# Layer A's turned probabilities: sixteen transfers inside the on-chip memory per half, and the products with v ahead of the next queries

## The chip, the cores and the metric

The kernel runs on one core of one Trainium2 chip. The metric is the device time of one execution in microseconds (us). The core has five engines that run their own instruction streams: TensorE (PE, matrix products), VectorE (DVE), ScalarE (ACT), GpSimd (POOL) and SyncE (SP, which here only issues transfers). Sixteen DMA engines move the data. Each engine takes its instructions in order, so an instruction that waits holds up all that stand behind it on the same engine.

## The reference

One layer A (dilated window attention, three groups) and one layer B (neighbourhood attention) on 512 rows of width 1024. The part that matters here is layer A's attention of each head:

```
logits = einsum('brhqd,brhkd->brhqk', qb, kb) * scale + bias
logits = where(valid, logits, NEG_INF)
mx = max(logits, axis=-1);  p = exp(logits - mx)
denom = sum(p, axis=-1)
out = einsum('brhqk,brhkd->brhqd', p, vb) / denom
...
y = sum(alpha * out over the three groups) * silu(gate);  x = x + y @ w_out
```

The probabilities p come out with the queries on the partitions. For the product with v the keys have to be on the partitions, so p is turned.

## The kernel before

Layer A works on eight pairs of heads (hc = 0 to 7, `NHC`). Two Python generators are woven into one program. `main` holds the projections: for each hc a fixed list of weight blocks, each 128 x 1024 float32 (512 KB), is loaded into one of nine buffers `wraw` (L256, on SP's queue), split into a rounded part `wh` (ACT, L133) and the rest `wl` (DVE or POOL in turns, L137), and multiplied in three products per block (PE, L286, `acc`). A block's half of 512 columns is a "job" here: 6 products for a mixed block, 12 for the blocks of the gate and of v. The projections of q and k are mixed from four blocks b11, b21, b12, b22 in a scheme with sums; some sums of weights are made by transfers that add to a buffer, issued from POOL (L184), and by POOL itself (L177). Each hc has 32 jobs: 0 to 3 b11, 4 and 5 gate, 6 to 9 b21, 10 to 13 b11 with b12 added to it, 14 to 17 a sum t2, 18 to 21 b22, 22 to 25 b12 with b22 added to it, 26 and 27 v, 28 to 31 t2 with b21 added to it. For the next hc they go on at 0.

`side` holds the attention: `q_a` (four groups of transposes of `rawq`, the projected queries and keys), `k_a` (`rawk`), `attn_a` (scores `log`, softmax `p`, turning, products with v `o`). PE's order is fixed where the generators weave: a clock that counts PE's work (`clock`) decides when `side` takes its next step, and `later_on` puts a job (a transfer) at a distance on that clock. The order on the other engines is made by a scheduler's own estimate of times; `keep_in_program_order` pins an instruction against others of its engine.

A pair of heads is done in two halves u = 0, 1 of 256 queries. For each half, DVE turns blocks of 32 x 32 within their 32 partitions (`turner.put`, L850, into the tile `tr`, of which there is one buffer). The blocks must then change partitions: block row a of 32 partitions, part b of the columns, goes to partitions 32b to 32b + 31. `turner.send` does it through DRAM: four writes `td<-tr` of 256 KB (L859), and 8500 units of the clock later four reads `pt<-td` of 256 KB (L863), 1300 units apart, all on SP's queue. Layer B uses the same class with 224 KB, for all but its last two pairs. When all reads of u = 1 are issued, `stamp` holds ("pt", hc, 1); 6000 units later `weigh` makes the products with v (`o<-pt`: 48 products), and `put_y` multiplies by the gate and stores y (`y_d<-gt`, L779).

For hc up to 6 the steps after the scores are: load the next biases (`bias_a`, L813 and L818), `v_a` (transposes of `vt`), `q_a(hc + 1)`, wait for ("pt", hc, 1), `weigh`. Before `main` allocates the next `rawq` it asks for `q_a` to have been done (`yield "q", hc - 1`). At hc = 6, y of the first pairs is read back (`yr<-y_d`, L798) into the buffer `tr`, and ACT rounds it (L804). hc = 7 turns its probabilities on PE and has no such transfers.

The lines that the scheduler and `order` name: a transfer on SP's queue waits for its buffers and also for the transfer eight places earlier on that queue.

Of the kernel before, what the change touches and what calls it, by code (L numbers as in the profile page):

```python
# [46 lines left out]
def tile_hybrid_encoder(  # L47
# [13 lines left out]
    nc = tc.nc  # L61
# [216 lines left out]
    clock = [0.0]  # L278
# [27 lines left out]
    def later_on(delay, job):  # L306

        timers.append((clock[0] + delay, job))
        timers.sort(key=lambda t: t[0])
# [529 lines left out]
    class turner:  # L839
# [12 lines left out]
        def send(self, dst, wait, pace, key=None):  # L852
# [15 lines left out]
            for b in range(4):  # L868
                later_on(pace * b, partial(write, b))
                later_on(wait + pace * b, partial(read, b))  # L870

    def attn_a(hc):
        e0, e12 = st.pop(("e", hc))
        q0h, q0l, q12, k0h, k0l = st.pop(("q", hc))
# [101 lines left out]
        if hc < NHC - 1:  # L976
            for u in range(2):
                turned = turner(512)
                turners.append(turned)
                for hd, t, pr in scores(u):  # L980
                    turned.put(pr, 512, 256 * hd + 128 * (t % 2))
                key = ("pt", hc, u)
                later_on(10000, partial(turned.send, pq[:, 2048 * u : 2048 * u + 2048], 8500, 1300, key))
                yield 9500
            if hc + 1 < NHC:
                st["e", hc + 1] = bias_a(hc + 1)
            yield from v_a(hc)
            yield from q_a(hc + 1)
            yield "wait", ("pt", hc, 1), 6000
            if hc < NHC - 2:  # L990
                put_y(hc, weigh(), True, False)
                yield
                return
            back = y_back(range(4), "tr")
            yield "wait", ("rawk", hc + 1), 0
            put_y(hc, weigh(), True, False)
            for n in range(4):
                y_split(back, n, n)
            yield "wait", ("q", hc + 1), 0
            back = y_back(range(4, NHC - 2), "rawq")  # L1000
            yield 4000
            for n in range(4, NHC - 2):
                y_split(back, n - 4, n)
        else:
            for u in range(2):
                held = scores(u)
                yield 4000
                for args in held:
                    turn_p(*args)
                    yield  # L1010
            yield from v_a(hc)
            yield "wait", ("gate", hc), 500
            stamp["ya", "turned"] = 0
            put_y(hc, weigh(), True, True)
            yield
# [386 lines left out]
```

## Time and profile before

| | |
|---|---|
| time, median of 3 runs | 948.82 us (945.91 to 950.09) |
| the profiled execution: its time | 949.64 us |
| its span, first to last instruction | 947.8 us |
| mean granted clock of TensorE | 0.951 |
| PE busy | 851.6 us, 90% |
| DVE, ACT, POOL busy | 613.8, 506.4, 354.3 us |
| moved by all transfers | 153.84 MB |
| HBM read, written | 126.41 MB, 26.40 MB |

Layer A's projections and attention take the span up to about 600 us, its output projection follows, and layer B runs from about 700 us. In a view of windows the row of a stretch gives its length, then for PE, PEld, DVE, ACT and POOL the busy time with the number of instructions, then the granted clock of TensorE, the share of DMA engine time, and GB/s. In a timeline a row is start, duration, engine, line, operation, output and inputs, and in brackets the idle time before it with what ended it. SPq is SP's queue: the time there is that of issuing.

### The profile page before, as it was taken

The numbers are of one execution on the slowest core, as the hardware profiler recorded it, in microseconds if no ns is written. First come the engines' busy times: TensorE is split into PE (matmuls) and PEld (weight loads), VectorE is DVE, ScalarE is ACT, GpSimd is POOL, SyncE is SP. The second block draws the span as 40 slices with busy tenths as digits, with TensorE's granted clock in tenths as the row PEclk, the third lists the DMA queues.
The fourth block names the chain that finished last, engine by engine and source line by source line (L and its number), as shares of the span: only waits on it lengthen the run. The fifth ranks groups of instructions, "written<-read, shape, count | busy, mean of one in ns | idle before, by whom it ended". The sixth has DMA issues, their size and how long they took to land.

```text
span 947.8 us, 15692 instructions
## 1 busy us (share of the span) xinstructions
PE 851.6 (90%) x5475; PEld 693.5 (73%) x5475; DVE 613.8 (65%) x1563; ACT 506.4 (53%) x1058; POOL 354.3 (37%) x328
## 2 busy tenths in 40 slices
PE   7957989996996996996996995999999999999998
PEld 5746767784774774775774774788999888888876
DVE  7776766872783684684585584753856776666743
ACT  6535654852752763663663663553546666544641
POOL 6346335534454443444453452411122223213411
PEclk9879999997997998997998998899999999999999
DMA  9252389698598488498498498126526554455212
GB/s 346 86 123 45 115 240 201 175 246 174 141 249 179 136 249 177 126 246 189 115 236 200 105 236 232 50 75 216 184 78 184 151 162 136 133 182 153 87 45 90
DMA packets 66911, 153.84 MB, mean 162 GB/s; under 512 B 7184, under 2 KB 24528, under 8 KB 66704
## 3 DMA queue, kind: packets, MB, share of 16 engines
q1 hardware_dynamic: 60496, 130.80, 46.8%
q0 software_dynamic: 6048, 22.02, 12.6%
q8 instruction: 43, 0.70, 0.3%
q14 instruction: 36, 0.29, 0.1%
q10 hardware_dynamic: 288, 0.01, 0.0%
HBM read 126.41 MB, written 26.40 MB: 161 GB/s over the span
## 4 chain that ended last, share of the span: by engine, by line
PE 49%; DMA 16%; ACT 12%; DVE 12%; issue 6%; POOL 3%; SPq 2%; DVEq 0%; ACTq 0%; POOLq 0%
PE acc L286 39%; DMA wraw<-in_w 10%; ACT wh L133 4%; PE o L286 4%; PE tp L290 3%; DMA td<-tr 3%; PE log L286 2%; ACT p L941 2%; ACT p L760 2%; DVE wl L137 2%; POOL wl L137 2%; ACT p L1198 1%; SPq L818 1%; DMA pt<-td 1%; DVE tr L850 1%
## 5 line engine op out<-in xcount | busy, mean ns | idle before, releaser
L137 POOL TENSOR_TENSOR wl<-wraw,wh 128x512 fp32r<-128x512 f32 (+1 forms) x167 | 221.3, 1334 | 391.1 <-ACT wh L133 370.5
L133 ACT CAST wh<-wraw 128x512 fp32r<-128x512 f32 (+1 forms) x360 | 211.8, 593 | 251.1 <-PE acc L286 243.1
L137 DVE TENSOR_TENSOR wl<-wraw,wh 128x512 fp32r<-128x512 f32 (+1 forms) x193 | 155.3, 808 | 159.0 <-ACT wh L133 155.9
L286 PE MATMUL acc<-wl,hn_h 128*128 128x384 f32 (+1 forms) x488 | 183.9, 377 | 45.4 <-POOL wl L137 44.7
L286 PE MATMUL acc<-wh,hn_h 128*128 128x384 f32 (+1 forms) x488 | 190.2, 390 | 3.0 <-DVE gt L1121 2.6
L286 PE MATMUL acc<-wh,hn_l 128*128 128x384 f32 (+1 forms) x488 | 182.1, 373 | 0.0
L286 PEld LDWEIGHTS acc<-wl,hn_h 128*128 128x128 f32 x488 | 95.3, 195 | 58.6 <-POOL wl L137 49.5
L286 PEld LDWEIGHTS acc<-wh,hn_h 128*128 128x128 f32 x488 | 95.3, 195 | 19.4 <-DVE gt L1121 4.2
L286 PEld LDWEIGHTS acc<-wh,hn_l 128*128 128x128 f32 x488 | 95.2, 195 | 10.2
L286 PE MATMUL acc<-wl,mix_h 128*128 128x512 f32 x224 | 90.5, 404 | 8.0 <-DVE wl L137 4.2
L286 PE MATMUL acc<-hn_h,wh 128*128 128x512 f32 x192 | 80.0, 417 | 11.7 <-ACT wh L133 11.4
L286 PE MATMUL acc<-wh,mix_h 128*128 128x512 f32 x224 | 88.8, 396 | 0.4 <-ACT wh L133 0.4
L286 PE MATMUL acc<-wh,mix_l 128*128 128x512 f32 x224 | 88.0, 393 | 0.0
L286 PE MATMUL acc<-hn_h,wl 128*128 128x512 f32 x192 | 76.1, 396 | 1.6 <-DVE wl L137 1.6
L286 PE MATMUL acc<-hn_l,wh 128*128 128x512 f32 x192 | 75.9, 395 | 0.0
L760 ACT ACTIVATE p<-p,mn 128x512 f32<-128x512 f32 (+3 forms) x128 | 70.9, 588 | 2.1 <-DVE mn L759 2.1
L184 POOL DMA_DIRECT2D wraw<-in_w x42 | 38.7, 996 | 82.4 <-DMA wraw<-in_w 77.2
L850 DVE STREAM_TRANSPOSE tr<-p 128x512 f32<-128x512 f32 (+1 forms) x80 | 54.9, 686 | 19.4 <-ACT p L760 14.3
L941 ACT ACTIVATE p<-p,mn 128x512 f32<-128x512 f32 (+1 forms) x64 | 44.9, 702 | 41.2 <-DVE mn L930 41.0
L286 PEld LDWEIGHTS acc<-wl,mix_h 128*128 128x128 f32 x224 | 42.4, 189 | 24.3 <-DVE wl L137 8.2
L286 PEld LDWEIGHTS acc<-hn_h,wh 128*128 128x128 f32 x192 | 36.6, 191 | 22.5 <-ACT wh L133 11.7
L372 DVE TENSOR_REDUCE ss<-sq 128x4 f32<-128x256 f32 (+1 forms) x96 | 47.3, 501 | 7.5 <-POOL sq L371 3.9
(158 smaller groups left out, 1470.7 us busy)
## 6 DMA issues: line engine op xcount, KB each, us to landing
wraw<-in_w SPq DMA_DIRECT2D x95, 512.0 KB
wraw<-in_w POOLq DMA_DIRECT2D x42, 512.0 KB, 7.9
wraw<-in_w SPq DMA_DIRECT2D x38, 384.0 KB
td<-tr SPq DMA_DIRECT2D x56, 256.0 KB
pt<-td SPq DMA_DIRECT2D x56, 256.0 KB
td<-tr SPq DMA_DIRECT2D x24, 224.0 KB
pt<-td SPq DMA_DIRECT2D x24, 224.0 KB
e<-l_d SPq DMA_DIRECT2D x32, 112.0 KB
```

Of the source, the lines that this page charges most:

```text
L133: nc.scalar.copy(h, raw)
L137: eng.tensor_sub(l, raw, h.bitcast(F32))
L184: lambda: nc.gpsimd.dma_start(dst.tile, src(), accum_op=ALU.add)
L286: nc.tensor.matmul(o, l, r, **kw)
L290: nc.tensor.transpose(o, i, ident)
L372: nc.vector.tensor_reduce(ss[:, i * ns : (i + 1) * ns], sq.rearrange("p (a b) -> p a b", b=64), axis=AX.X, op=ALU.add)
L760: nc.scalar.activation(pr, pr, AF.Copy, scale=mn[:, 3:4])
L818: nc.sync.dma_start(e12[:, 2 * hd + g, :], bass.AP(l12_d.tensor, l12_d.offset + h * 512 + 256 * g + 31, [[0, 4], [-1, 32], [1, 224]]),)
L850: nc.vector.transpose(dst, src[:, :n].rearrange("p (i b k) -> p i b k", b=4, k=32))
L941: nc.scalar.activation(row, row, AF.Exp, bias=mn[:, 1:2], scale=-1.0, accum_out=mn[:, 2:3])
L1198: nc.scalar.activation(pr[:, o : o + n], pr[:, o : o + n], AF.Exp, bias=mn[:, 0:1], scale=-1.0, accum_out=mn[:, 2:3])
```

## The change

Layer A no longer calls `turner.send`. A new method `move` moves each 32-partition block of `tr` straight to its place in `pt`, on-chip memory to on-chip memory: 4 steps of 4 transfers, each 32 partitions x 512 float32 (64 KB), 1500 clock units between the steps. ("pt", hc, u) is stamped when the last step is issued, so 14500 units after the half began instead of 22400. For hc < 6 `weigh` and `put_y` now come before `q_a(hc + 1)`; for hc = 6 the order is as it was. Layer B keeps `send`.

```diff
+        def move(self, dst, pace, key):
+            run = self.run
+            place = dst.rearrange("p (a x) -> p a x", a=4)
+
+            def step(n):
+                for b in range(4):
+                    a = (b + n) % 4
+                    src = self.t[32 * a : 32 * a + 32, b * run : b * run + run]
+                    tc.keep_in_program_order(nc.sync.dma_start(place[32 * b : 32 * b + 32, a, :], src))
+                self.left -= 1
+                if not self.left:
+                    stamp[key] = clock[0]
+
+            for n in range(4):
+                later_on(pace * n, partial(step, n))
...
-                later_on(10000, partial(turned.send, pq[:, 2048 * u : 2048 * u + 2048], 8500, 1300, key))
+                later_on(10000, partial(turned.move, pq[:, 2048 * u : 2048 * u + 2048], 1500, key))
                 yield 9500
             if hc + 1 < NHC:
                 st["e", hc + 1] = bias_a(hc + 1)
             yield from v_a(hc)
-            yield from q_a(hc + 1)
             yield "wait", ("pt", hc, 1), 6000
             if hc < NHC - 2:
                 put_y(hc, weigh(), True, False)
                 yield
+                yield from q_a(hc + 1)
                 return
+            yield from q_a(hc + 1)
             back = y_back(range(4), "tr")
```

How it moves instructions, at three places. On PE, after the transposes of `vt` (the difference, first pair of heads; `o` are the products with v, `acc` the projections, six of them a job, `tp<-ident,rawq` the first group of the next queries' transposes):

```order
 L286 MATMUL acc<-wl,hn_h 128x512
 L286 MATMUL acc<-wh,hn_l 128x512
+L286 MATMUL o<-pt,rawk 64x4x32 x16
+L286 MATMUL o<-pt,v_1312 64x2x128 x2
+L286 MATMUL o<-pt,v_1312 64x256 x6
+L286 MATMUL acc<-wh,hn_h 128x512
+L286 MATMUL acc<-wl,hn_h 128x512
+L286 MATMUL acc<-wh,hn_l 128x512
+L286 MATMUL acc<-wh,hn_h 128x512
+L286 MATMUL acc<-wl,hn_h 128x512
+L286 MATMUL acc<-wh,hn_l 128x512
 L290 MATMUL tp<-ident,rawq 128x128 x4
```

The products with v stood four jobs and four groups of transposes later; now they come one job after the transposes of `vt`. What follows on the side (the next `rawk` transposes and both halves' scores) stands 15 products later among the projections, and from the scores of u = 1 to the products with v there are 111 projection products instead of 150.

On SP's queue, from the second half's transfers to the store of y, around the fourth pair. Before (`wraw_3390` to `wraw_3493` are the blocks b21, b21, b22, b22 of the coming hc, `wraw_3661` and `wraw_3706` its two blocks b12):

```order
L863 DMA pt_98<-td_3235 32x4x512
L859 DMA td_3344<-tr_3152 128x512
L256 DMA wraw_3390<-in_w 128x1024
L859 DMA td_3344<-tr_3152 128x512
L256 DMA wraw_3413<-in_w 128x1024
L256 DMA wraw_3452<-in_w 128x1024
L863 DMA pt_98<-td_3344 32x4x512 x4
L256 DMA wraw_3493<-in_w 128x1024
L256 DMA wraw_3661<-in_w 128x1024
L256 DMA wraw_3706<-in_w 128x1024
L779 DMA y_d_91<-gt_3069 128x512
```

Now (the same blocks are `wraw_3439`, 3469, 3508, 3549, and b12 `wraw_3718` and `wraw_3749`):

```order
L881 DMA pt_98<-tr_3228 32x512 x4
L256 DMA wraw_3439<-in_w 128x1024
L881 DMA pt_98<-tr_3228 32x512 x8
L256 DMA wraw_3469<-in_w 128x1024
L256 DMA wraw_3508<-in_w 128x1024
L881 DMA pt_98<-tr_3228 32x512 x4
L256 DMA wraw_3549<-in_w 128x1024
L256 DMA wraw_3718<-in_w 128x1024
L256 DMA wraw_3749<-in_w 128x1024
L779 DMA y_d_91<-gt_3028 128x512
```

The loads of b12 are still the last two before the store of y, behind all transfers of the second half. The first half's sixteen transfers stand together after the loads of v and of the two b11 (in the kernel before, its four writes stood after the load of v).

On POOL, at the jobs 0 to 3 of an hc. Before (`wraw_3298` and `wraw_3323` are b11, `wraw_3661` and `wraw_3706` b12):

```order
L618 COPY vt_3490<-vt_3490 128x64
L184 DMA wraw_3661<-in_w 128x1024
L137 TENSOR_TENSOR wl_3523<-wraw_3298,wh_3522 128x512
L184 DMA wraw_3706<-in_w 128x1024
L184 DMA wraw_3298<-in_w 128x1024
L137 TENSOR_TENSOR wl_3593<-wraw_3323,wh_3592 128x512
```

Now (b11 `wraw_3347` and `wraw_3375`, b12 `wraw_3718` and `wraw_3749`):

```order
L618 COPY vt_3546<-vt_3546 128x64
L137 TENSOR_TENSOR wl_3579<-wraw_3347,wh_3578 128x512
L184 DMA wraw_3347<-in_w 128x1024
L184 DMA wraw_3718<-in_w 128x1024
L184 DMA wraw_3749<-in_w 128x1024
L137 TENSOR_TENSOR wl_3668<-wraw_3375,wh_3667 128x512
```

The subtraction of job 1 now stands ahead of the transfers that add to b12; that of job 3 stands behind both of them.

## The prediction

> **What bounds the kernel now.** I read the page's busy times and slices first, then PE's waits, then windows and timelines around the stalls.
>
> ```profile
> PE 851.6 (90%) x5475; PEld 693.5 (73%) x5475; DVE 613.8 (65%) x1563; ACT 506.4 (53%) x1058; POOL 354.3 (37%) x328
> ...
> PE   7957989996996996996996995999999999999998
> DMA  9252389698598488498498498126526554455212
> ```
>
> PE is busy 90% of the span. In layer A it dips to 4 to 6 tenths every third slice, and the DMA row is at 9 just there. So PE sets the end, but for some waits of a fixed period. The view of PE's waits from 100 to 600 us:
>
> ```profile
> PE acc L286 <- POOL wl L137: 47.6, 11, 9.3
> PE acc L286 <- ACT wh L133: 11.8, 2, 11.4
> ```
>
> Eleven waits, 47.6 us, are on a subtraction of POOL, and two, 11.8 us, on a rounding of ACT. Six windows hold nearly all of it:
>
> ```profile
> 190.00:224.00 34.00, 24.66 (x115) 19.69 (x113) 22.71 (x49) 14.85 (x26) 10.81 (x11) 0.92 0.89 223
> 257.00:298.00 41.00, 31.20 (x142) 24.57 (x140) 29.01 (x61) 21.56 (x40) 14.58 (x15) 0.94 0.84 219
> 331.00:372.00 41.00, 31.65 (x144) 24.93 (x142) 29.48 (x64) 22.01 (x41) 14.35 (x15) 0.96 0.87 217
> 405.00:445.00 40.00, 30.94 (x141) 24.36 (x139) 28.65 (x61) 21.19 (x38) 14.83 (x15) 0.94 0.88 217
> 480.00:520.00 40.00, 30.64 (x137) 23.99 (x136) 27.41 (x58) 20.06 (x36) 15.78 (x17) 0.94 0.87 213
> 560.00:600.00 40.00, 26.77 (x112) 20.82 (x112) 23.65 (x39) 17.22 (x28) 13.72 (x10) 0.79 0.74 203
> ```
>
> Length less PE's time is 9.3, 9.8, 9.4, 9.1 and 9.4 us for five pairs of heads (46.9 us together) and 13.2 us for the last window. The timelines of POOL and PE show one of the five:
>
> ```profile
> 354.71 1.67 POOL L137 TENSOR_TENSOR wl<-wraw,wh 128x512 fp32r<-128x512 f32 x1 [3.92 <-ACT wh L133]
> 370.12 0.87 POOL L184 DMA_DIRECT2D wraw<-in_w  x1 [13.10 <-DMA wraw<-in_w]
> 370.73 1.55 POOL L137 TENSOR_TENSOR wl<-wraw,wh 128x512 fp32r<-128x512 f32 x1
> ```
>
> ```profile
> 357.07 0.66 PE L290 MATMUL tp<-ident,vt 128*128 128x128 f32 x4 [0.21 <-POOL vt L618]
> 362.98 0.48 PE L286 MATMUL acc<-wh,hn_h 128*128 128x512 f32 x1
> 372.34 0.79 PE L286 MATMUL acc<-wl,hn_h 128*128 128x512 f32 x1 [8.88 <-POOL wl L137]
> ```
>
> PE stops at 363.5 because the `wl` of job 1 comes at 372.3. POOL did not lack its input; it stood 13.1 us at L184, a transfer that adds to b12 and must first see b12 loaded, with job 1 behind it. SP's queue shows why b12 is late, a window view of the DMA share what it waits behind:
>
> ```profile
> 321.98 0.33 SPq L256 DMA_DIRECT2D wraw<-in_w  x1
> 328.10 0.33 SPq L256 DMA_DIRECT2D wraw<-in_w  x1
> ...
> 351.94 4.45 SPq L863 DMA_DIRECT2D pt<-td  x4
> 356.50 3.40 SPq L256 DMA_DIRECT2D wraw<-in_w  x3
> ```
>
> ```profile
> 310.00:320.00 10.00, 10.00 (x115) 8.04 (x113) 5.40 (x22) 6.01 (x15) 3.71 (x2) 1.00 0.01 4
> 360.00:365.00 5.00, 3.46 (x20) 2.60 (x18) 4.86 (x13) 3.24 (x7) 0.00 (x0) 1.00 1.05 211
> ```
>
> The three loads at 356.50 are b22 and the two b12. They go out behind the four reads `pt<-td`, into DMA engines that are 0.87 busy over the window's 41 us (1.05 from 360 to 365) and stood idle from 310 to 320 (0.01), until SP's next load at 321.98 had a buffer. About 11 us later the first b12 has landed. So the stall is one of DMA time: what is taken out of the queue ahead of b12 shortens it.
>
> A stall costs more than its length, since the clock is low after it (the chain of waits, one stall):
>
> ```profile
> 298.11 2.50 PE acc L286 x5
> 300.61 0.85 PE tp L290 x4
> 303.90 3.62 PE o L286 x48
> 310.23 1.40 PE acc L286 x6
> ```
>
> Five products take 2.50 us, where six take 1.40 later (five: 1.17), and the four transposes behind them run at the same low clock, so about half of their 0.85 is lost as well. 1.3 + 0.4 and a little of what follows: I take 2 us a stall, 10 us for five.
>
> **The change, part by part.**
>
> *The write to DRAM goes.* Per half 1.05 MB less pass the DMA engines. Layer B's writes of the same kind, in two windows of an emptier stretch:
>
> ```profile
> 749.00:750.00 1.00, 1.00 (x7) 0.75 (x5) 0.86 (x6) 0.00 (x0) 0.00 (x0) 1.00 0.86 326
> 753.00:754.00 1.00, 1.00 (x8) 1.00 (x7) 0.63 (x2) 0.43 (x1) 0.00 (x0) 1.00 0.88 209
> ```
>
> At 326 GB/s the write leg is 3.2 us of all engines, 6.4 us per pair of heads. The read leg (the second row holds the reads into 32 partitions and a load) runs nearer 209 GB/s, 5.0 us a half. No row shows a transfer from the on-chip memory to itself. Bounds: it costs like the write, 3.2 us a half, or its 64 KB cost SP as the dearest small issue does (below). I take the read's 5.0 us, the row nearest to it, since both write to 32 partitions; then the move is the old read, and the write is saved.
>
> *Issuing.* Sixteen issues a half replace eight:
>
> ```profile
> L859 SPq DMA_DIRECT2D td<-tr x80: 319/424/1568, 113.0 to 861.0; - x80
> ```
>
> ```profile
> 332.57 5.58 SPq L818 DMA_DIRECT2D e<-l_d  x4
> ```
>
> At the writes' median of 0.42 us they cost SP 6.8 us a half; the old eight took about as much with their waits (4.45 us for four reads above). The upper bound is the row of the biases, four issues in 5.58 us, 1.4 each, 22 us a half. I take 0.4: a move is one plain run of 2 KB per partition, as the write is. For landing I take 3 us from layer B, where a read goes out as soon as its write has landed (first write to first read, 3.1 us):
>
> ```profile
> 747.81 2.17 SPq L859 DMA_DIRECT2D td<-tr  x4
> 750.87 0.94 SPq L863 DMA_DIRECT2D pt<-td  x2
> ```
>
> *Does b12 come in time?* In times of the stall above: the second half's scores stand 15 products (3.5 us at 0.23) later among the projections, and its four transposes now also stand behind two more subtractions and a pair of evacuations.
>
> ```profile
> 336.68 0.70 DVE L850 STREAM_TRANSPOSE tr<-p 128x512 f32<-128x512 f32 x1
> ```
>
> They ended at 337.4; now about 342.5 (3.5, and an estimated 1.6 for what stands ahead). SP then has 16 moves and six loads: 8.4 us of issuing at 0.4 or less, and for the DMA engines 5.0 us and 3.1 MB at 326 GB/s, 9.6 us. From 342.5 that is 357, and with 3 us for landing 360; the second b12's buffer is free when POOL's row 354.71 ends, at 356.4, which fits. So b12 has landed at about 360 and not 370. PE would ask for it later than now: job 3, not job 1, stands behind it, with the products with v (3.62 us, row 303.90) ahead of them: 363.5 + 3.6 - 0.4 (one group of transposes fewer, half of 0.85) + 2 x 1.8 = 370. POOL needs two issues of 0.87 and a subtraction of 1.3 after the landing, 363. Spare: 7 us, of which a shorter period eats part. I forecast this stall gone, less 1 us a pair that I leave for the uneven order of loads.
>
> *The products with v come earlier.* They wait on PE itself, and all that follows on PE waits with them. One job after row 357.07 they stand at about 359; the last four moves go out at about 350.5, with twelve moves and three loads before them, and land by 354. Spare 5 us. What hid a late `pt` so far was the stall.
>
> *Later scores.* The softmax of a first half now falls wholly among jobs of 1.4 us, where part of it lay beside the gate's slow ones (12 products, 2.8 us).
>
> ```profile
> 312.69 0.61 ACT L133 CAST wh<-wraw 128x512 fp32r<-128x512 f32 x1
> 319.97 0.60 ACT L133 CAST wh<-wraw 128x512 fp32r<-128x512 f32 x1
> ```
>
> Between two roundings ACT was 7.3 us away, and PE lived on jobs rounded ahead. It had 2.1 us (9 products of the gate) more cover than it will have. I charge 1.5 us for each of six pairs, 9 us; bounds 0 (the scheduler put a rounding in between) and 4 us a pair.
>
> *The first half's moves and `tr`.* The second half's transposes reuse `tr` once the moves have left it. For the first pair that wait exists already:
>
> ```profile
> 124.27 0.71 DVE L850 STREAM_TRANSPOSE tr<-p 128x512 f32<-128x512 f32 x1 [4.39 <-DMA td<-tr]
> ```
>
> It stays, at 4 us: 16 moves after 113 us are no faster than four writes into full DMA engines. In later pairs the moves go out from 328 (row 328.10, the second b11) and have landed by 328 + 6.4 + 3 = 337, before the transposes at 339.
>
> *The end of layer A.* The last window's 13.2 us are ACT's rounding behind `yr`:
>
> ```profile
> 574.47 0.52 SPq L798 DMA_DIRECT2D yr<-y_d  x1
> ...
> 592.70 0.80 PE L286 MATMUL acc<-hn_h,wh 128*128 128x512 f32 x1 [11.41 <-ACT wh L133]
> ```
>
> ```profile
> ACT y_h L804 <- DMA yr<-y_d: 16.6, 2, 13.1
> ```
>
> `yr` went out after the reads and the loads, at 574.47, and landed some 13 us later. Now nothing but the sixteen moves and three loads stands before it, and ACT's L804 stands four roundings later. I take 10 of 13.2 us and 2 us of low clock.
>
> **Sum**, against the profiled span of 947.8: 46.9 + 10 + 10 + 2 = 68.9 us go; 9 for the softmax and 5 x 1 for the rest of the waits come back: 947.8 - 68.9 + 14 = 893. The time of that execution was 949.64, 1.8 above its span and 0.8 above the median, so the median forecast is 894 us. If all waits go and nothing comes back: 947.8 - 46.9 - 10 - 13.2 - 2 = 876, time 877.
>
> **Rivals.** *Half of it (chance 0.24).* The transfers crowd the DMA engines as before, since the idle 10 us at 310 stay and the moves start later than the writes did. For it: the engines were 0.87 busy over 41 us and only 6.4 us of work leave. Against it: PE also asks 7 us later. Then each of five stalls keeps about 5 us and its low clock, and the last keeps half: 894 + 5 x (4 + 2) + 6 = 930.
>
> *Small transfers hold the queue (0.16), slower than before.* If a move costs SP or its eight places 1.4 us, as the biases' issues do, the second half's moves take 22 us from 342.5: the last of them, with loads in between, goes out at about 366 and lands at 369, against 359 asked. PE stops 10 us at `o`, in place of 9.4. It gets worse by the first half's moves, which end at 328 + 22 = 350 and hold DVE's transposes, put at 342.5, and the `wl` behind them: 7.5 us less some 4 us of jobs ahead. So from 0.7 us a move the stalls are as now, and at 1.4 each of six pairs pays about 4 us more: 949 + 24 = 973. Against it: 0.42 for writes of four times the rows. The Trainium skill, page "DMA: Bandwidth & Descriptors", section "Rules for kernel authors", speaks for this rival: it advises to coalesce many small transfers, and says that under 64 KB one pays mostly overhead; its section "Bandwidth" gives 0.95 us for a 64 KB load from HBM, by which sixteen in a row would be 15.2 us a half, an estimate. No run here shows a transfer of 64 KB alone, and by the rows' rate of 326 GB/s it would be 0.2 us.
>
> *No change (0.05).* The DMA work saved is hidden behind SP's waits for buffers, and b12 comes when it came. Against it: its buffers are free at 356.4, and it landed 13 us later.
>
> **How the numbers follow.** Forecast 0.55, half 0.24, slow transfers 0.16, none 0.05. The forecast's own range is 876 to 915 (4 us a pair for the softmax, 15 more, and a few us of waits). The range reaches into the half case: 872 to 930, leaving out the slow case, none, and the worse part of the half. A difference under 0.5% (4.7 us) can't be told from none here: faster 0.79 (the first two cases), same 0.05, slower 0.16.
>
> **What would show it.** Right: L184's wait on POOL falls from 13 us to under 4 in pairs 2 to 6; PE's idle per period falls from 9.4 to under 4; no wait of `o`; HBM written falls by 14.7 MB; sixteen moves issued in under 8 us. Wrong: a wait of PE before `o` on a transfer; SP's rows for the moves above 0.7 us each; DVE's transposes waiting for `pt<-tr`; PE waits on ACT's `wh` above 2 us per pair in the softmax.

## The result, and the profile after

The change makes the kernel slightly slower: 956.65 us median (20 runs) against 948.87 us for the kernel before on the same chip (20 runs), a ratio of 1.0065 [1.0041, 1.0088]. Here and below a median is over all executions of a kernel, and a ratio leaves out those in a slower state of the chip (4 of the changed kernel's 20). The forecast was 894 us. The profiled execution took 959.71 us, its span 957.6 us.

From the page of the changed kernel: the busy times, the slices of PE and DMA, and what HBM moved.

```profile
PE 862.1 (90%) x5475; PEld 701.2 (73%) x5475; DVE 643.6 (67%) x1563; ACT 506.4 (53%) x1058; POOL 356.0 (37%) x328
...
PE   7957975989988979988998898999999999999998
...
DMA  9253448168267567466555644526525554565212
...
HBM read 111.73 MB, written 11.72 MB: 129 GB/s over the span
```

14.7 MB less are written to HBM (11.72 for 26.40 MB), as the change says. The DMA row no longer has a 9 in every third slice, and PE's dips to 5 or 6 tenths in every third slice are gone, but for one of 5 in the seventh slice, the first pair's. In their place PE is at 8 tenths in every second or third slice. The chain of waits has 10% of SP's queue in it (2% before):

```profile
PE 43%; DVE 18%; ACT 11%; SPq 10%; DMA 8%; issue 7%; POOL 2%; DVEq 0%; ACTq 0%; POOLq 0%
```

PE's waits over the whole span of the changed kernel (sum in us, times, the longest):

```profile
PE acc L286 <- DVE wl L137: 20.2, 9, 3.0
PE tp L290 <- DVE rawk L388: 17.1, 7, 4.9
PE o L286 <- DMA pt<-tr: 11.8, 1, 11.8
PE acc L286 <- POOL wl L137: 10.8, 14, 0.9
PE o L286 <- DMA wraw<-in_w: 4.8, 2, 2.8
PE o L286 <- issue: 4.5, 2, 2.5
PE acc L286 <- ACT wh L133: 3.7, 8, 0.5
```

The nine-microsecond stalls behind POOL's `wl` are gone: its longest wait is 0.9 us. Three groups came instead, mostly of short ones: on DVE's `wl`, on `rawk`, and before the products with v (`o`), 11.8 + 4.8 + 4.5 = 21.1 us. Two of them, `o` and DVE's `wl`, lead to the sixteen moves. The rows of the moves, the wait of the transposes for `tr`, and SP's timeline (two first halves, one second half, and the read of `yr`) show it:

```profile
L881 SPq DMA_DIRECT2D pt<-tr x224: 507/589/2642, 111.3 to 598.9; - x112
```

```profile
DVE tr L850 <- DMA pt<-tr: 19.3, 6, 3.8
```

```profile
268.50 12.10 SPq L881 DMA_DIRECT2D pt<-tr  x16
...
286.24 3.87 SPq L881 DMA_DIRECT2D pt<-tr  x4
...
290.94 7.27 SPq L881 DMA_DIRECT2D pt<-tr  x8
...
299.38 2.41 SPq L881 DMA_DIRECT2D pt<-tr  x4
...
341.20 11.99 SPq L881 DMA_DIRECT2D pt<-tr  x16
...
601.25 0.33 SPq L798 DMA_DIRECT2D yr<-y_d  x1
```

One move costs SP 0.59 us by the median, which is 9.4 us for sixteen. Sixteen in a row take 12.1 us (0.76 each): a transfer can go out only when the one eight places before has landed, and some have to wait for that. The second half's sixteen go out from 286.2 to 301.8, with three loads between, and PE asks for them at once. The rows of PE are those of the first pair and of this one:

```profile
153.89 3.68 PE L286 MATMUL o<-pt,rawk 128*64 128x128 f32 x32 [11.84 <-DMA pt<-tr]
```

```profile
304.94 3.52 PE L286 MATMUL o<-pt,rawk 128*64 128x128 f32 x32 [2.85 <-DMA wraw<-in_w]
```

At 304.94 PE has stood 2.85 us, and it starts 3 us after the last move was issued; the label names another transfer that ended there. The first 32 of these products then take 3.52 us, at a granted clock of 0.55 from 304.9 to 308.5, where the kernel before needs 1.97 us for the same 32 at 303.83. So a late `pt` costs twice, by the wait and by the low clock behind it.

### The profile page after: what moved, and what is told of

Same layout as the page of the kernel before. It is cut to its first block, busy times and chain, and to the rows that moved or that the text cites. A ratio compares the mean times of both kernels' runs of the same rounds, so it can differ in the third digit from the quotient of the medians.

```text
span 957.6 us, 15831 instructions
## 1 busy us (share of the span) xinstructions
PE 862.1 (90%) x5475; PEld 701.2 (73%) x5475; DVE 643.6 (67%) x1563; ACT 506.4 (53%) x1058; POOL 356.0 (37%) x328
## 3 DMA queue, kind: packets, MB, share of 16 engines
HBM read 111.73 MB, written 11.72 MB: 129 GB/s over the span
## 4 chain that ended last, share of the span: by engine, by line
PE 43%; DVE 18%; ACT 11%; SPq 10%; DMA 8%; issue 7%; POOL 2%; DVEq 0%; ACTq 0%; POOLq 0%
PE acc L286 34%; SPq L881 8%; PE o L286 4%; PE tp L290 4%; DMA wraw<-in_w 3%; DVE wl L137 3%; ACT wh L133 3%; ACT p L958 2%; DMA e<-l_d 2%; DVE tr L850 2%; DVE na L121 2%; DVE rs L122 2%; PE log L286 2%; DVE rawk L388 2%; ACT p L760 1%
## 5 line engine op out<-in xcount | busy, mean ns | idle before, releaser
L137 POOL TENSOR_TENSOR wl<-wraw,wh 128x512 fp32r<-128x512 f32 (+1 forms) x167 | 214.1, 1282 | 470.7 <-ACT wh L133 442.1
L137 DVE TENSOR_TENSOR wl<-wraw,wh 128x512 fp32r<-128x512 f32 (+1 forms) x193 | 148.9, 774 | 110.9 <-ACT wh L133 109.0
L286 PE MATMUL acc<-wl,hn_h 128*128 128x384 f32 (+1 forms) x488 | 179.0, 367 | 1.5 <-DVE wl L137 0.7
L286 PE MATMUL acc<-wh,hn_l 128*128 128x384 f32 (+1 forms) x488 | 179.0, 367 | 0.0
L286 PE MATMUL acc<-wl,mix_h 128*128 128x512 f32 x224 | 92.9, 415 | 29.6 <-DVE wl L137 19.4
L286 PEld LDWEIGHTS acc<-wh,hn_h 128*128 128x128 f32 x488 | 93.5, 192 | 19.6 <-DVE gt L1139 4.2
L286 PEld LDWEIGHTS acc<-wh,hn_l 128*128 128x128 f32 x488 | 93.1, 191 | 10.3
L286 PE MATMUL acc<-wh,mix_h 128*128 128x512 f32 x224 | 91.2, 407 | 3.3 <-ACT wh L133 3.3
L286 PE MATMUL acc<-wh,mix_l 128*128 128x512 f32 x224 | 90.1, 402 | 0.0
L850 DVE STREAM_TRANSPOSE tr<-p 128x512 f32<-128x512 f32 (+1 forms) x80 | 52.5, 676 | 27.4 <-DMA pt<-tr 19.3
L184 POOL DMA_DIRECT2D wraw<-in_w x42 | 36.7, 874 | 55.8 <-DMA wraw<-in_w 40.5
L286 PEld LDWEIGHTS acc<-wh,mix_h 128*128 128x128 f32 x224 | 43.5, 194 | 17.0 <-ACT wh L133 6.4
```

The source lines that it names most:

```text
L137: eng.tensor_sub(l, raw, h.bitcast(F32))
L184: lambda: nc.gpsimd.dma_start(dst.tile, src(), accum_op=ALU.add)
L286: nc.tensor.matmul(o, l, r, **kw)
L850: nc.vector.transpose(dst, src[:, :n].rearrange("p (i b k) -> p i b k", b=4, k=32))
```

## The experiments

Theories at the start: 1, *issuing* (sixteen transfers hold SP 12 us a half, and what stands behind them is late); 2, *the order* (products with v directly behind `vt` lose what covered a late `pt`, and the next scores stand later); 3, *bytes* (the transfers load the DMA engines whatever their number); A, *POOL's standing* at L184 is what the stalls of the kernel before cost. Later ones came up on the way: C, DVE is slow at `rawk` because of where L184 puts POOL's work; 2a and 2b split theory 2 (the order costs only where `pt` is late, or by itself through the later scores), and 2c says how (the first half's moves fall behind weight loads). A ratio is to the kernel before, on the same chip; times of different rows come from several chips, whose medians of the kernel before lie between 947.8 and 950.6 us.

| run | order | pieces of a half | L184 | us | ratio |
|---|---|---|---|---|---|
| before | old | through DRAM | free | 949 | 1 |
| changed | new | 16 transfers | free | 956.65 | 1.0065 [1.0041, 1.0088] |
| order_only | new | through DRAM | free | 964.33 | 1.0161 [1.0132, 1.0190] |
| move_only | old | 16 transfers | free | 932.59 | 0.9807 [0.9770, 0.9844] |
| move_again | old | 16 transfers | free | 932.66 | 0.9845 [0.9786, 0.9904] |
| later_o | new, o 3000 later | 16 transfers | free | 947.38 | 0.9972 [0.9941, 1.0002] |
| two_queues | new | 16, 8 of them from ACT | free | 973.93 | 1.0268 [1.0239, 1.0297] |
| moves8 | new | 8 of 128 KB | free | 1000.66 | 1.0546 [1.0513, 1.0579] |
| before_pin | old | through DRAM | held | 960.98 | 1.0129 [1.0082, 1.0176] |
| after_pin | new | 16 transfers | held | 965.48 | 1.0180 [1.0145, 1.0214] |
| move_only_pin | old | 16 transfers | held | 946.50 | 0.9968 [0.9935, 1.0001] |
| move_gap | old, u = 1 later | 16 transfers | free | 924.39 | 0.9653 [0.9562, 0.9744] |
| gap_pin | old, u = 1 later | 16 transfers | held | 937.53 | 0.9888 [0.9840, 0.9935] |
| move8_pin | old | 8 of 128 KB | held | 902.33 | 0.9509 [0.9480, 0.9539] |
| move8_new | new | 8 of 128 KB | held | 973.16 | 1.0263 [1.0213, 1.0312] |
| copy8_pool | old | 8, ACT 4, POOL 4 | held | 917.20 | 0.9676 [0.9621, 0.9732] |
| copy8_act | old | 8, ACT 8 | held | 920.26 | 0.9701 [0.9651, 0.9750] |
| copy4_act | old | 12, ACT 4 | held | 900.70 | 0.9501 [0.9448, 0.9554] |
| copy4_new | new | 12, ACT 4 | held | 960.04 | 1.0120 [1.0066, 1.0175] |
| copy4_free | old | 12, ACT 4 | free | 922.72 | 0.9697 [0.9657, 0.9737] |

The three kernels with pieces of 128 KB (moves8, move8_pin, move8_new) leave the blocks in other places, so their products with v are of wrongly placed probabilities; they stand here for their time alone.

### The two parts apart

move_only and move_again (one kernel, measured twice) put the products with v back where they were:

```diff
             yield from v_a(hc)
+            yield from q_a(hc + 1)
             yield "wait", ("pt", hc, 1), 6000
             if hc < NHC - 2:
                 put_y(hc, weigh(), True, False)
                 yield
-                yield from q_a(hc + 1)
                 return
-            yield from q_a(hc + 1)
```

> The sixteen transfers stay, the products with v stand behind the next queries' transposes again, as before the change. Theory 1 (issuing: sixteen transfers take SP some 12 us per half, so the second half's transposes wait for tr, and b12 is loaded late): the wait of tr on pt<-tr stays near 19 us in all, and the time stays within 4 us of the changed kernel's 956.7. Theory 2 (the order: the products with v stand where nothing covers a late pt, and the next pair's work is late behind them): the waits before o on a transfer (17 us in all) and those of tp on rawk (17 us) fall under 5 us each, and the time falls under 945. Theory 3 (the transfers themselves, by bytes on the DMA engines): as theory 1, and DMA's share in the stretch of the moves stays above 0.9.

> The kernel with the sixteen transfers and the old order once more, for its profile: time 930 to 936, as measured. Theory 2 (the order took the gain) expects that PE waits under 5 us in all before o, that the stall at tp on rawk falls from 17 us to under 5, and that the 9 us stalls of the kernel before are mostly gone; theory 1 (issuing) that DVE waits for tr on pt<-tr near 19 us as in the changed kernel, and that this is covered here.

order_only makes the opposite edit in the kernel before, with 5500 for 8500 in its `send`.

> The turned probabilities go through DRAM as before, with 5500 in place of 8500 units from the first write to the first read (with 8500 the products could not stand ahead), and the products with v stand ahead of the next queries' transposes. Theory 1 (issuing): within 5 us of the kernel before, 948.9, since SP's work is as before. Theory 2 (the order): PE waits before o, 3 us a pair or more, and stalls behind rawk as in the changed kernel, 2 us a pair; the time is 955 or more. Theory 3 (bytes): slower than the changed kernel, as the write leg's 3.2 us a half are back on the way to o.

The transfers alone gain 16 us (932.6), the order alone loses 15 (964.3). So what the change lost is in its second, small part: with the moves in place it costs 956.65 - 932.6 = 24 us. PE's waits of move_again:

```profile
PE acc L286 <- DVE wl L137: 30.1, 9, 5.1
PE tp L290 <- DVE rawk L388: 18.6, 9, 4.9
...
PE o L286 <- PE acc L286: 0.6, 1, 0.6
```

Against the changed kernel's rows the wait before `o` is gone (0.6 for 21.1 us), the one on DVE's `wl` has grown (30.1 for 20.2), and that on `rawk` stays. Theory 2's first half holds, its part on `rawk` does not: with L184 where the scheduler puts it, that stall is there in both orders when the moves are used, and in order_only, with the new order but through DRAM, there is none in the pairs (4.9 us in all, as in the kernel before). Theory 1 is right about `tr`, which waits 24.5 us in move_again, not less than in the changed kernel, and wrong about the time, which it put within 4 us of 956.7. In order_only PE waits 19.0 + 15.8 us before `o`, on reads that come back from DRAM, so an early `o` waits with either way of turning. POOL's stalls are mostly gone there too (10.8 us in three waits), though L184 still stands 10.5 to 13.0 us in each pair: the order takes them away without b12 coming sooner.

later_o leaves the new order and asks for `o` 3000 units later:

```diff
-            yield "wait", ("pt", hc, 1), 6000
+            yield "wait", ("pt", hc, 1), 9000
```

> The changed kernel with the products with v 9000 in place of 6000 units behind the last transfers' issue, still ahead of the next queries' transposes. Theory 2a (what the new order costs is the wait before o): the waits before o (21 us in the changed kernel) fall under 4 us and the time to 935 to 945. Theory 2b (what it costs is that the next queries' transposes and with them the next scores stand later, so that the scaling of rawk and the transposes into tr fall on other work): o no longer waits, but rawk and wl of DVE wait as in the changed kernel or longer, and the time is 950 to 962.

947.4 us, 9 us better, but `o` still waits 17.9 us in all (7.4 of it in the first pair). The edit was too small to take the wait away, and the run doesn't decide between 2a and 2b.

### What sixteen transfers cost

moves8 moves the same bytes in eight transfers; two_queues gives every second transfer to ACT's queue:

```diff
-                for b in range(4):
-                    a = (b + n) % 4
-                    src = self.t[32 * a : 32 * a + 32, b * run : b * run + run]
-                    tc.keep_in_program_order(nc.sync.dma_start(place[32 * b : 32 * b + 32, a, :], src))
+                for b in range(2):
+                    src = self.t[32 * n : 32 * n + 32, 2 * b * run : 2 * b * run + 2 * run]
+                    to = slice(2048 - 1024 * (b + 1), 2048 - 1024 * b)
+                    tc.keep_in_program_order(nc.sync.dma_start(dst[96 - 32 * n : 128 - 32 * n, to], src))
```

```diff
-                    tc.keep_in_program_order(nc.sync.dma_start(place[32 * b : 32 * b + 32, a, :], src))
+                    tc.keep_in_program_order((nc.scalar if b % 2 else nc.sync).dma_start(place[32 * b : 32 * b + 32, a, :], src))
```

> Eight transfers of 32 partitions x 1024 (128 KB) in place of sixteen of 64 KB, the same bytes; the blocks land in other places, so the products with v are of wrongly placed probabilities. Theory 1 (issuing): SP needs 6 us per half in place of 12; the waits of tr and of o fall by more than half, and the time falls to 935 to 948. Theory 2 (the order): the waits before o fall as well, but the stalls behind rawk stay, 950 to 956. Theory 3 (bytes): eight transfers take as long to land as sixteen, the waits of tr and o are as in the changed kernel, and so is the time, 956.7 within 3.

> Every second transfer of a half is issued from ACT's queue, the others from SP's; the rest as in the changed kernel. Theory 1 (issuing): SP needs 5 to 6 us per half, the waits of tr and o fall by more than half; ACT pays 8 issues of about 0.6 us a half, which its roundings ahead cover in part: 940 to 952. Theory 2 (the order): as the changed kernel less the waits before o, 950 to 956. Theory 3 (bytes): the waits of tr and o stay, and ACT's issues come on top: 957 to 970.

Both are slower than every theory had them. Their waits suggest why, PE's of moves8 first, ACT's of two_queues second:

```profile
PE tp L290 <- POOL vt L618: 38.1, 7, 7.5
```

```profile
ACT wh L133 <- DMA pt<-tr: 72.1, 17, 7.8
```

In moves8 the scheduler, which orders the other engines by its own estimate, now puts a transfer that adds to b12 (L184) ahead of the copy of `vt` on POOL, and PE waits for `vt`. In two_queues an issue on ACT waits like one on SP, and the roundings `wh` stand behind it, 72.1 us. The Trainium skill, page "DMA: Bandwidth & Descriptors", section "Rules for kernel authors", says that spreading transfers over queues only saves issue time; here it moved the wait to an engine that has other work.

So the place of L184 had to be fixed before the number of transfers could be told. before_pin, after_pin and move_only_pin hold it where it is written, some twelve jobs later, in the kernel before, in the changed one and in move_only:

```diff
-                lambda: nc.gpsimd.dma_start(dst.tile, src(), accum_op=ALU.add)
+                lambda: tc.keep_in_program_order(nc.gpsimd.dma_start(dst.tile, src(), accum_op=ALU.add))
```

> The kernel before, with the transfers that add to a weight block (L184) held in their written place on POOL: those that add to b12 then stand some twelve jobs later, behind the subtractions. Theory A (the 9 us stalls are POOL's standing at L184 for b12's load): the stalls of POOL wl go from 48 us to under 8, and the time to 890 to 910. Theory B (the stalls are the load itself, late by crowded DMA engines): the waiting moves to b12's own products or to wh, and the time stays above 930.

> The changed kernel with the same hold on L184. Theory 2 (the order): the waits before o, on rawk and on DVE's wl are not POOL's and stay, 945 to 957. Theory C (DVE is held while POOL works; L184 ahead of job 3's subtraction pushes POOL's work into the scaling of rawk): the stall at tp on rawk falls from 17 us to under 6, and the time to 930 to 945.

> Sixteen transfers, the old order, and L184 held in place. Theory A: what is left of POOL's standing goes as well; faster than move_only, 890 to 915. If it is no faster than before_pin, the transfers bring nothing that holding L184 does not; if it is faster by 5 us or more, the DRAM leg's DMA time counts beside it.

Theory A, on which the prediction's sum stood as well, forecast 890 to 910 us for before_pin. POOL no longer stands (its waits at L184 on loads fall from 77.2 to 4.4 us), and the kernel before gets 1.3% slower. PE's waits of before_pin, and one row of SP's queue in the kernel before and in before_pin, in the same pair:

```profile
PE o L286 <- DMA wraw<-in_w: 29.7, 3, 11.0
PE o L286 <- DMA pt<-td: 14.9, 2, 9.6
...
PE o L286 <- issue: 9.4, 1, 9.4
```

```profile
257.33 5.90 SPq L818 DMA_DIRECT2D e<-l_d  x4
```

```profile
267.35 13.14 SPq L818 DMA_DIRECT2D e<-l_d  x4
```

54 us before `o`: the wait has moved from POOL's `wl` to the turned probabilities. Part of this POOL's stall had hidden. In before_pin `o` starts 13 to 14 us after the last read is issued; in the kernel before it would have been asked for some 12 us after it without the stall, so by an estimate from these figures about 2 us a pair would have been left. The larger part comes with the hold: SP stands longer at the loads of the next biases, ahead of the reads (13.1 us for 5.9 in the two rows), and the last read goes out 60 to 62 us after the products with v of the pair before, for 52 to 54. So before_pin refutes theory A's forecast, but what the stall alone was worth it does not tell. after_pin lost 9 us too, and its waits on `rawk` stayed at 17.5 us, against theory C; in move_only_pin they are 4.9 us, one wait ahead of layer A's pairs, so with L184 held the order does decide that stall. In move_only_pin the waiting is on DVE's `wl` (49.7 us), behind transposes that wait for `tr` (37.1 us).

With L184 held in both, move8_pin (moves8's edit) against move_only_pin tells the number of transfers:

> As move_only_pin (old order, L184 held in place), with eight transfers of 128 KB in place of sixteen of 64 KB; the blocks land in other places, so the products with v are of wrongly placed probabilities. Theory 1 (issuing): SP needs 6 to 7 us per half, tr's wait on pt<-tr falls from 37 us to under 15, PE's waits on DVE's wl from 50 us to under 20, and the time from 946 to 905 to 925. Theory 3 (the transfers' bytes): tr waits as long, and the time stays within 5 us of 946.

```profile
PE acc L286 <- DVE wl L137: 49.7, 9, 8.3
```

```profile
DVE tr L850 <- DMA pt<-tr: 37.1, 6, 7.6
```

```profile
245.47 15.33 SPq L881 DMA_DIRECT2D pt<-tr  x16
```

```profile
PE acc L286 <- DVE wl L137: 7.7, 2, 7.4
```

```profile
DVE tr L850 <- DMA pt<-tr: 6.1, 1, 6.1
```

```profile
241.60 4.97 SPq L881 DMA_DIRECT2D pt<-tr  x8
```

The first three rows are move_only_pin's, the last three move8_pin's: eight transfers go out in 4.97 us where sixteen took 15.33, `tr` waits 6.1 us in all for 37.1, `wl` 7.7 for 49.7, and the time falls by 44 us with the same bytes moved. So the number of transfers counts and theory 3 falls. Issue time is not all of it: of the 10.4 us between the two rows, eight issues of 0.59 us are 4.7. The rest is waiting for transfers eight places before, and in move_only_pin these share the DMA engines with POOL's transfers that add (L184). Three of those go out from 250.8, when eight moves are out, and POOL's queue has 68.0% of the engines' time from 250.4 to 260.8; in move8_pin the moves are out at 246.57 and POOL's three start at 246.94. With L184 free, in move_again, the same sixteen took 12.55 us, 4.95 of them for the first eight.

move_gap and gap_pin give the moves time in another way, `yield 12000 if u == 0 else 9500` for `yield 9500` between the halves, in move_only and move_only_pin.

> Sixteen transfers, the old order, and 12000 in place of 9500 units from the first half's scores to the second's. Theory 1 (issuing: SP is 12 us at the first half's transfers, and the second half's transposes stand behind them on DVE with a wl behind those): the wait of tr on pt<-tr falls from 24.5 us to under 8, PE's waits on DVE's wl from 30 us to under 12, and the time from 932.6 to 915 to 925. Against it (the scores only get later, and what follows waits instead): 930 or more.

> move_gap with L184 held in its written place. Theory 1: tr's wait falls from 37 us to under 20, and since rawk did not wait in move_only_pin, the time falls below that of move_gap or to 905 to 920. Against it (held L184 makes the second half's transfers, and with them b12, later, so DVE waits elsewhere): 930 to 945.

By the medians both gained 8 to 9 us, though the four runs of move_gap lie between 909 and 928 us, a spread wider than the gain, and its ratio rests on two of them. `tr` waited on: 20.5 us on `pt<-tr` in move_gap, 23.8 in gap_pin, with as much again put down to loads in gap_pin. The expected cause isn't shown by these two, and why gap_pin is faster stays open.

### Fewer transfers, the other pieces copied by engines

Four of a half's sixteen pieces stay on their partitions, and an engine can copy them, or other pieces too:

```diff
+                    to = place[32 * b : 32 * b + 32, a, :]
+                    if n == 0:
+                        nc.scalar.copy(to, src)
+                    else:
-                    tc.keep_in_program_order(nc.sync.dma_start(place[32 * b : 32 * b + 32, a, :], src))
+                        tc.keep_in_program_order(nc.sync.dma_start(to, src))
```

This is copy4_act, in move_only_pin; copy8_pool adds `nc.gpsimd.tensor_copy(to, src)` for n = 1, copy8_act `nc.scalar.copy(to, src)`; copy4_free is copy4_act without the hold.

> As copy8_act with four copies on ACT and twelve transfers. Theory 1 (issuing, in proportion): SP needs 9 to 10 us per half, and the time lies between move_only_pin's 946 and copy8_act's, 920 to 935. Against it: as move_only_pin, 940 to 948.

> As move_only_pin (old order, L184 held), but of the sixteen pieces of a half four (those that stay on their partitions) are copied by ACT and four by POOL (32 partitions over), and eight go by SP's transfers; the output is whole. Theory 1 (issuing): as with the eight large transfers SP needs 5 to 8 us per half, tr's wait on pt<-tr falls under 15 us, and the time is 902 to 925. Against it (the copies cost ACT, POOL and, beside POOL, DVE what SP saves): 935 or more.

> The same with all eight copies on ACT, four us of its time in a row in each half. Theory 1: 902 to 925, nearer the low end if POOL's copies hold DVE up in copy8_pool. Against it (roundings on ACT come late behind the copies): PE waits on wh 2 us or more in each half, 925 to 945.

> copy4_act without the hold on L184, so old order, twelve transfers, four copies. The first L184 for b12 then stands ahead of the copy of vt on POOL. If POOL's standing at L184 for b12 costs here (theory A), PE waits for vt or for POOL's wl 3 us or more a pair, and the time is 915 to 960; if b12 is in time by now, 898 to 905.

copy4_act runs in 900.7 us, 5% under the kernel before and 56 us under the changed one, faster than both. A copy takes ACT 0.62 us. From its page the busy times:

```profile
PE 842.5 (94%) x5475; PEld 683.5 (76%) x5475; DVE 613.8 (68%) x1563; ACT 537.9 (60%) x1114; POOL 358.8 (40%) x328
```

PE is busy 94% of the span, and twelve transfers of a first half go out in 8.79 us (the row stands in the next section). The version was expected between move_only_pin and the kernels with eight, and it beats these; copying four more pieces didn't pay. At the end of layer A copy8_act has a wait of 11.2 us on `vt` (copy4_act one of 7.0 on ACT's `v`), and its pairs take 66.5 us for 64.5, by the last five stores of y of each; which of the added copies costs what was not taken apart. Without the hold the same kernel needs 922.7 us and PE waits 23.7 us on POOL's `wl` (6.2 with it): L184 ahead of subtractions costs 22 us here, as theory A said of the kernel before, where holding it gained nothing.

### The order with early transfers

move8_new is move8_pin, copy4_new is copy4_act, each with the changed kernel's order.

> move8_pin (eight transfers of 128 KB, L184 held, wrongly placed probabilities) with the changed kernel's order. Theory 1 alone (all that the changed kernel loses is the issuing time): within 6 us of move8_pin's 902.3. Theory 2a (the order puts o ahead of late transfers, and only late transfers make it cost): the same, 902 to 908, and no wait before o. Theory 2b (the order itself costs, by the later scores): 912 to 925, o does not wait, and rawk and wl of DVE wait 2 us a pair or more.

> copy4_act with the changed kernel's order. If the order costs only where transfers are late (theory 2a), twelve early transfers make it harmless: 900 to 908. If the order puts the first half's transfers behind three weight loads on SP's queue, as in move8_new (theory 2c), tr's wait on pt<-tr comes back at 20 us or more in all, DVE's wl is late behind it, and the time is 940 to 975.

The order costs 71 us with eight transfers and 59 us with twelve, with under 2 us of waits before `o`: by itself, and more than in the changed kernel. The rows of one pair, SP and DVE of copy4_act first, then of copy4_new, with the shares of the DMA queues from 260 to 270 us (q0 is POOL's, q1 holds SP's), POOL's adding transfers, and one stall of PE:

```profile
239.81 8.79 SPq L885 DMA_DIRECT2D pt<-tr  x12
```

```profile
234.44 0.71 DVE L850 STREAM_TRANSPOSE tr<-p 128x512 f32<-128x512 f32 x1 [0.18 <-ACT p L760]
...
239.04 0.70 DVE L850 STREAM_TRANSPOSE tr<-p 128x512 f32<-128x512 f32 x1
...
252.10 0.71 DVE L850 STREAM_TRANSPOSE tr<-p 128x512 f32<-128x512 f32 x1 [1.14 <-ACT wh L133]
```

```profile
245.33 11.60 SPq L256 DMA_DIRECT2D wraw<-in_w  x3
258.15 11.01 SPq L885 DMA_DIRECT2D pt<-tr  x12
```

```profile
250.16 0.71 DVE L850 STREAM_TRANSPOSE tr<-p 128x512 f32<-128x512 f32 x1 [0.46 <-ACT p L760]
...
257.38 0.70 DVE L850 STREAM_TRANSPOSE tr<-p 128x512 f32<-128x512 f32 x1
...
274.40 1.90 DVE L850 STREAM_TRANSPOSE tr<-p 128x512 f32<-128x512 f32 x3 [7.20 <-DMA e<-l_d]
```

```profile
q0 software_dynamic: 465, 1.71, 87.2%
q1 hardware_dynamic: 423, 0.62, 19.6%
```

```profile
256.52 0.87 POOL L184 DMA_DIRECT2D wraw<-in_w  x1
...
259.11 1.78 POOL L184 DMA_DIRECT2D wraw<-in_w  x2 [0.30 <-POOL wl L137]
...
262.93 0.88 POOL L184 DMA_DIRECT2D wraw<-in_w  x1
```

```profile
276.92 0.80 PE L286 MATMUL acc<-wl,mix_h 128*128 128x512 f32 x1 [6.32 <-DVE wl L137]
```

In the old order the first half's transposes end at 239.7, and the second half's find `tr` free at 252.1. In the new order the scores stand later among the projections, and the transposes take 7.9 us instead of 5.3 (to 258.1). The moves follow at once, at 258.15, and take SP 11.0 us instead of 8.8. Three loads of 512 KB stand just ahead of them on SP's queue, but the last is issued by 256.9, before the transposes end, and all of q1, moves included, has only 19.6% of the DMA engines' time from 260 to 270 us. POOL's queue has 87.2%: its four adding transfers go out from 256.5 to 263.8, beside the moves. In copy4_act only one goes out among the moves, at 243.45, and the next two at 247.83, when the moves are nearly out.

DVE waits 7.2 us at the transposes, the `wl` behind them comes late, and PE stops 6.3 us. (The label names a load of biases; what these transposes write is `tr`, and the last packet of the moves ends at 273.7 in the trace, just before their start at 274.40.) So it isn't the early `o` but its effect on what follows that costs here. Theory 2c had the time right, and the wait of the transposes for `tr` (13.6 us under its own label, 48.9 with the loads named in its place). Its cause isn't borne out in this pair, where the moves meet POOL's adding transfers and not SP's loads. How much of the 59 us these make, and how much the later and longer softmax, was not tried apart.

## Why the prediction was wrong

- **What bounds the kernel: half right.** The five stalls and their place on POOL were read rightly, and they went; from the second pair on L184 stands 2.0 to 4.8 us at b12 in place of 13. But "what is taken out of the queue ahead of b12 shortens it" took one waiting engine for the bound, and the sum counted the 46.9 us as if nothing could wait in their place. order_only and before_pin lose most of the same stalls and are 1.6% and 1.3% slower: in both the wait moved to `o`.
- **The write to DRAM goes: right.** 14.7 MB less written; DMA share no longer 9 tenths.
- **Issuing: wrong, the first failed step.** "I take 0.4" for a move, from writes that go out four at a time, gave 6.4 us a half. It is 0.59 us, and 0.76 in a row of sixteen, 12 us a half. What a row of sixteen adds, the wait for the transfer eight places before, got no price of its own in the sum, though the rival below it names the eight places. The rival "small transfers hold the queue" had the point from which the gain is gone, 0.7 us, and that is where the measured value lies; the waits it named, of PE at `o`, of DVE's transposes and at the `wl` behind them, are the ones that show (21.1, 19.3 and 20.2 us). The Trainium skill, page "DMA: Bandwidth & Descriptors", spoke for that rival. Its section "Rules for kernel authors" (coalesce many small transfers) agrees with move8_pin, where eight of 128 KB for sixteen of 64 KB made 44 us. The estimate of 15.2 us a half, worked out from its section "Bandwidth", stands beside 12.1 us in the changed kernel and 15.3 in move_only_pin, though the page's figure is for moving a load and these are SP's times.
- **The products with v come earlier: wrong, the second failed step.** "Spare 5 us" rested on moves issued by 350, in 8 us with the loads between them; in the changed kernel the second half's take 15.6 us with its loads, and `o` waits 21.1 us in all. The forecast gave the order no cost of its own beyond later scores. Taken apart, it costs 24 us with these moves, 19 with L184 held, 15 through DRAM, and 59 to 71 with fewer transfers and L184 held.
- **Later scores: right in direction, mis-sized and misplaced.** I charged 1.5 us a pair for ACT. Waits of PE on `wh` are only 3.7 us in all. The cost is on DVE, as far as the runs show: later and longer transposes and a wait for `tr`, in copy4_new beside POOL's adding transfers. What of this makes it so dear stays open.
- **`tr` free in later pairs: wrong.** The moves were to go out from 328 and to have landed by 337; in that pair they go out from 341 to 353, and `tr` waits in six places, 19.3 us.
- **End of layer A: half right.** ACT's wait behind `yr` falls from 16.6 to 3.5 us, but `yr` itself goes out at 601 instead of 574 us, since the last of the moves ahead of it goes out at 599.5, where the last read went out at 574.4.
- **The sum.** Of the 63 us between 894 and 956.65, 24 are the order's (956.65 to 932.6). Of the other 39, 32 came back in copy4_act, with twelve transfers and L184 held (932.6 to 900.7). Twelve transfers alone give 10 of them (copy4_free, 922.7), and the hold alone loses 14 (move_only_pin, 946.5). The two work only together, so the 39 us can't be shared out between issuing and the place of L184. That copy4_act comes near the forecast is no credit to it: it is another kernel, with fewer transfers, L184 held and the old order.

## What to carry to other kernels

Cost small transfers by their issue time times the number in a row, not by their bytes alone, and count separately those beyond the number that may be under way at once, which wait for whatever else loads the DMA engines. When one stall is taken away, ask which wait stood hidden behind it, and whether its input is ready earlier at all. An edit that only moves work to an earlier place moves all that follows against the loads on the shared queue; test it apart from the edit it comes with.

## What was not expected of the hardware

The issue time on SP is the same for the two sizes tried: 0.59 us median for 64 KB pieces (the changed kernel's row above) and for 128 KB pieces, by move8_pin's row of the moves:

```profile
L881 SPq DMA_DIRECT2D pt<-tr x112: 507/588/2010, 113.1 to 525.8; - x112
```

Small operations of DVE are held while POOL works. DVE's and POOL's timelines of the changed kernel, at the scaling of `rawk`:

```profile
240.71 0.17 DVE L121 SCALAR_TENSOR_TENSOR na<-na,nv 128x16 f32<-128x16 f32 x1
240.92 1.25 DVE L122 SCALAR_TENSOR_TENSOR rs<-na,rs 128x16 f32<-128x16 f32 x1
...
242.42 2.27 DVE L121 SCALAR_TENSOR_TENSOR na<-na,nv 128x16 f32<-128x16 f32 x1
```

```profile
240.86 1.28 POOL L137 TENSOR_TENSOR wl<-wraw,wh 128x512 fp32r<-128x512 f32 x1 [1.21 <-ACT wh L133]
242.22 2.44 POOL L177 TENSOR_TENSOR wraw<-wraw 128x1024 f32<-128x1024 f32 x1
```

An operation on 128 x 16 numbers takes 0.17 us alone (the first row); the next two shown last 1.25 and 2.27 us and end within 0.05 us of POOL's operation beside them. The Trainium skill, page "SBUF — State Buffer", section "Who interferes with whom", says that a DVE instruction with two inputs in SBUF contends with a GpSimd instruction that reads SBUF, over a pair of ports that is locked by one of them; these rows agree. The 48 operations `na<-na,nv` average 471 ns in the changed kernel and 213 before. That the 2.1 us stalls at `tp` behind `rawk` come from this is not shown: in move_only_pin and copy4_act, without those stalls, they average 192 and 235 ns, but in copy4_free, which has none either, 487.
